# Moving the token transposes into the mixer and cutting the first layer's modulation sums into 128x256 pieces

## The chip, the cores and the metric

One NeuronCore of a Trainium2 chip runs the whole program in one launch. The metric is device time in microseconds (us), the median of three runs. The engines are named as in the profile: PE (TensorE), DVE (VectorE), ACT (ScalarE), POOL (GpSimd) and SP (SyncE, which here issues most of the DMAs). Each engine executes its own list of instructions strictly in order.

## The reference

Two transformer layers work on 256 context tokens and 1024 latent tokens of width 1024, all in float32. The part that the change touches:

```python
x = x + ml[2] * mix_l                      # mix_l = recurrent mixer's output @ w_out
x = x + ml[5] * _conv_ffn(_modulate(_rms(x), ml[3], ml[4]), ffn_w_up[i], ffn_conv[i], ffn_w_down[i])
ctx = ctx + mc[2] * mix_c                  # the same for the context, in the first layer only
ctx = ctx + mc[5] * _conv_ffn(_modulate(_rms(ctx), mc[3], mc[4]), ...)
# ml, mc = split(silu(cond) @ mod_w[i] + mod_b[i], 6): six vectors of 1024 for each condition
```

## The kernel before

The program keeps tokens as columns. Its stages follow each other: a start that normalises the tokens; a **mixer** (four delta-rule heads, four gated-linear heads, up to about 960 us); the **output projection** of the mixer (about 962 to 1111 us); a feed-forward block for the context tokens (`fg<-hx`, from 1115 us); one for the latent tokens; then the second, attention layer. The tokens are cut in three chunks: chunk 0 is the context (256 columns), chunks 1 and 2 are latent (512 columns each).

The order on each engine is not written by hand. The program is recorded in source order, and a scheduler places each instruction by a time line of its own; tile pools (a pool with n buffers of a tag makes the n+1st tile wait for the first one's readers) and true dependencies are its limits.

*Mixer.* Projections (`pj`) fill PE between chains: per delta head `kk` (`pskk`), a 30-step `inverse` on DVE, and `levels` (`py`, `px`, `pxt`: short matmuls with a DVE step between them). `dn_step` walks the recurrence (`p`, `vn`, `r`). `merge(h8)` takes a finished head `o` (`o_d`, from DRAM scratch `o_scr`), squares it on ACT (`msq`), scales it on DVE (`mss`), transposes it on PE (`pmt`), gates it (`mg`) and stores it in `m_scr`. `merge(3)` is the last.

*Output projection* (`if True:` block from L1250). `m_in` loads the merged heads: for chunk 0 straight into `m`, for chunks 1 and 2 through `mt`, split into a high part (ACT, `m1h`, `m2h`) and a low part (DVE, `m1l`, `m2l`). `x_in` loads 128 tokens of 4 KB rows (`st`), transposes them on PE (`xtr`) and copies them into the residual `xT` on ACT and DVE. For each chunk and each of eight output tiles `dt`, a 512 KB weight tile is loaded (`st<-in_rec_w_out_dram`, L1303); chunk 0 multiplies it as it is (`po<-m,st`), chunks 1 and 2 split it (`woh` on ACT, `wol` on POOL) and run three products. DVE adds the result into `xT`. The head order `KORD` puts head 3 last.

*Modulation sums.* After each chunk `mod_acc(mp, pd, "d", 0, (4, 3, 5)[ci], (0, 1), 0, 1024)` computes one of the vectors 4, 3, 5 of layer 0 for both conditions: eight 512 KB weight tiles `mw` are loaded by SP, and DVE multiplies and adds them into two accumulators (`macc`, 128x1024). PE then sums over partitions (`mps`). After chunk 1 `rms_mod` makes `hx`, the context's normalised and modulated input of the feed-forward block: squares (ACT `rm_sq`), sums (DVE `rm_rs`, PE and DVE `rm_cs`), the power on POOL, a diagonal (`rm_dg`), a broadcast matmul, a product (DVE `rm_sq`), and a scale and shift that is dealt out by `scale_shift`: rows 0 to 3 to ACT, 4 and 5 to POOL, 6 and 7 to DVE. The modulation of layer 1 is already done in 128x256 pieces by `mod_chain`, through POOL's DMA queue with six `mw` buffers.

Of the kernel before, what the change touches and what calls it, by code (L numbers as in the profile page):

```python
# [9 lines left out]
F32 = mybir.dt.float32  # L10
# [9 lines left out]
KD = 8  # L20
NCTX = 256
NLAT = 1024
NT = NCTX + NLAT
# [47 lines left out]
def kernel(  # L71
# [33 lines left out]
    def pool(stack, name, bufs, psum=False, side=None):  # L105
        kw = {"space": PSUM} if psum else {}
        return stack.enter_context(tc.tile_pool(name=name, bufs=bufs, reuse_waits="tile", side=side, **kw))
# [33 lines left out]
    m_scr = dr.tile([8, 128, NT], F32, name="m_scr")  # L141
    aq_scr = dr.tile([2, 8, 128, NLAT], F32, name="aq_scr")
    x0_scr = dr.tile([2, 128, KD, NCTX], F32, name="x0_scr")

# [345 lines left out]
    with loop:  # L490
# [248 lines left out]
        def gatef(h8):  # L739
            gate_p(h8, lv, "ktk")  # L740

        bc8 = ac.tile([128, 2, 8], F32, name="bc8")
        dma(bc8[:, 0], dn_dt_bias[0].rearrange("a b -> (a b)").partition_broadcast(128))
# [57 lines left out]
        dn_run(1)  # L801
        kk(1)
        q_tok(1)
        inverse(1)
# [12 lines left out]
        pend += [(1, n) for n in range(NB)]  # L817
        kk(2)
        q_tok(2)
        inverse(2)  # L820
# [14 lines left out]
        dn_run(1)  # L835
        kk(3)
        q_tok(3)
        inverse(3)
# [237 lines left out]
    def load(p, src):  # L1076
        st = p.st.tile([128, KD, 128], F32, tag="st", name="st")
        dma(st, src)
        return st
# [178 lines left out]
    if True:  # L1258
# [4 lines left out]
        with ExitStack() as po:  # L1263
            hC = pool(po, "hC", 1, side="right")
            tmp = pool(po, "tmpc", 1)
            fc.st = pool(po, "fstc", 2)
            fw = Ffn()
            fw.st = pool(po, "fstw", 2)
            mi = pool(po, "mi", 4)
            wo = pool(po, "wo", 5)  # L1270
            mp = pool(po, "mpc", 1)
            mhl = {}
            def x_in(g):
                src = ctx_in[0, g:g + 128] if g < NCTX else x[0, g - NCTX:g - NCTX + 128]
                ci, o = (0, g) if g < NCTX else ((g - NCTX) // 512 + 1, (g - NCTX) % 512)
                xin = load(fc, src.rearrange("p (k m) -> p k m", m=128))
                for hf in range(2):
                    ps = pd.tile([128, 4, 128], F32, tag="d", name="xtr")
                    for k in range(4):
                        T.transpose(ps[:, k], xin[:, hf * 4 + k], ident)  # L1280
                    evac(hf, xT[ci][:, hf * 4:hf * 4 + 4, o:o + 128], ps)

            xs_ = iter(range(0, NT, 128))
            def m_in(ci):
# [7 lines left out]
                for k in KORD:  # L1292
# [3 lines left out]
                    tt(V, ml_[:, k], mt[:, 0:n], mh[:, k].bitcast(F32), ALU.subtract)  # L1296
            for ci in (0, 1, 2):
                m_in(ci)
            for _ in range(6):
                x_in(next(xs_))  # L1300
            for ci in (0, 1, 2):
                t0, n = CHUNKS[ci]
                d = 1 if ci == 0 else 0  # L1303
                if ci not in (0, 1, 2):
                    m_in(ci)
                for dt in range(KD):
# [11 lines left out]
                    stt(V, xT[ci][:, dt], ps[:, 0:n], mcol(0, d, 2)[:, dt:dt + 1], xT[ci][:, dt], ALU.mult, ALU.add)  # L1318
                    for _ in range({(0, d): 1 for d in range(2, 6)}.get((ci, dt), 0)):
                        x_in(next(xs_))  # L1320
                dump(f"xmix{ci}", xT[ci])
                mod_acc(mp, pd, "d", 0, (4, 3, 5)[ci], (0, 1), 0, 1024)
                if ci == 1:
                    hx = h0.tile([128, KD, NCTX], F32, tag="m0l", name="hx")
                    rms_mod(tmp, pd, "d", xT[0], NCTX, mcol(0, 1, 4), mcol(0, 1, 3), hx, None, w=128)
        if stop == "C":
# [356 lines left out]
```

## Time and profile before

| | |
|---|---|
| median of 3 runs (3437.09 to 3443.26) | 3440.48 us |
| the profiled execution's own time | 3433.85 us |
| its span | 3432.1 us |
| PE, DVE, POOL, ACT busy | 93%, 70%, 45%, 38% of the span |
| granted TensorE clock, mean | 0.964 of full speed |

The profile is one execution. "Busy" for PE includes the modelled tail of pipelined matmuls. The page cuts the span in 40 slices of 85.8 us; the slice from 944 us is one of three where PE's digit is 7, and the one where the DMA's is highest (8, 261 GB/s read and written).

### The profile page before, as it was taken

The page shows a single profiled execution, that of the slowest core. Times are in us where ns is not written, and L with a number is a line of the kernel's source. Part 1 is how long each engine was busy: PE and PEld are TensorE (multiplying, and loading weights), DVE is VectorE, ACT ScalarE, POOL GpSimd, SP SyncE. Part 2 cuts the span into 40 slices and gives each one's busy share as a digit, 9 for nine tenths or more (in the row PEclk, how much of TensorE's full clock was granted, in tenths as well). Part 3 has the DMA queues.
Part 4 walks back from the last instruction along what each step waited for, and adds up shares of the span by engine and source line. Part 5 has one row for each costly group of instructions (what it writes and reads, how often), then busy time and mean ns, then how long its engine had stood idle before and what let it go on. Part 6 is the DMA issues. An engine that isn't in the chain of part 4 may idle for free.

```text
span 3432.1 us, 47550 instructions
## 1 busy us (share of the span) xinstructions
PE 3184.6 (93%) x16708; PEld 2661.1 (78%) x16708; DVE 2414.4 (70%) x4177; ACT 1308.3 (38%) x2982; POOL 1542.5 (45%) x1459
## 2 busy tenths in 40 slices
PE   7987988899979999999999988989999799999998
PEld 4776877777768888788888778978788678887877
DVE  5567467568777875777676775577787667777677
ACT  4434233654321222333332324556356433333333
POOL 2232231223215332656555535753554555555554
PEclk9998999999989999999999999999999899999999
DMA  5445444645686664211212121330331011111211
GB/s 184 115 120 161 135 130 133 180 146 171 189 261 191 187 193 135 80 41 53 59 50 59 41 70 59 111 102 26 100 101 35 25 54 51 56 44 53 59 49 71
DMA packets 438508, 350.14 MB, mean 102 GB/s; under 512 B 57556, under 2 KB 385470, under 8 KB 437758
## 3 DMA queue, kind: packets, MB, share of 16 engines
q1 hardware_dynamic: 429054, 321.93, 31.5%
q0 software_dynamic: 9216, 25.18, 2.3%
q8 instruction: 132, 2.16, 0.3%
q14 instruction: 106, 0.87, 0.1%
HBM read 286.25 MB, written 60.76 MB: 101 GB/s over the span
## 4 chain that ended last, share of the span: by engine, by line
PE 64%; DVE 18%; DMA 6%; ACT 4%; POOL 3%; issue 3%; SPq 1%; DVEq 0%; ACTq 0%; POOLq 0%
PE fg L157 6%; PE fg L155 6%; PE fg L156 6%; PE fg L1220 4%; PE fd L156 4%; PE fd L157 4%; PE fd L155 4%; PE fd L1230 2%; DVE st L94 2%; PE pj L155 2%; PE pj L156 2%; PE pj L157 2%; PE apo L155 2%; PE apo L157 2%; PE apo L156 2%
## 5 line engine op out<-in xcount | busy, mean ns | idle before, releaser
L103 DVE SCALAR_TENSOR_TENSOR xT<-fd,mod,xT 128x512 f32<-128x512 f32 (+1 forms) x432 | 291.0, 694 | 201.9 <-PE fd L157 172.7
L155 PE MATMUL pj<-hhi,whi 128*128 128x512 f32 (+1 forms) x696 | 260.9, 375 | 21.2 <-ACT raw L525 13.4
L156 PE MATMUL fd<-gl,dh 128*128 128x512 f32 (+1 forms) x688 | 266.7, 388 | 6.5 <-DVE gl L94 6.4
L157 PE MATMUL fd<-gh,dl 128*128 128x512 f32 (+1 forms) x688 | 266.0, 387 | 0.0
L155 PE MATMUL fd<-gh,dh 128*128 128x512 f32 (+1 forms) x688 | 262.6, 392 | 0.5 <-ACT gh L1155 0.3
L156 PE MATMUL pj<-hlo,whi 128*128 128x512 f32 (+1 forms) x696 | 257.6, 370 | 1.2 <-DVE hlo L94 1.2
L157 PE MATMUL pj<-hhi,wlo 128*128 128x512 f32 (+1 forms) x696 | 257.1, 369 | 0.0
L94 DVE TENSOR_TENSOR st<-st 128x512 f32<-128x512 f32 x176 | 211.1, 1200 | 51.3 <-POOL s1l L94 38.7
L103 DVE SCALAR_TENSOR_TENSOR macc<-mw,sc,macc 128x256 f32<-128x256 f32 (+1 forms) x322 | 212.4, 690 | 28.3 <-DMA mw<-in_mod_w_dram 26.8
L94 POOL TENSOR_TENSOR dl<-sd,dh 128x256 fp32r<-128x256 f32 x168 | 158.7, 960 | 106.0 <-ACT dh L160 105.9
L94 POOL TENSOR_TENSOR wlo<-wst,whi 128x512 fp32r<-128x512 f32 x58 | 76.7, 1322 | 265.2 <-ACT whi L160 259.6
L100 POOL TENSOR_SCALAR P<-P,rc 128x512 f32<-128x512 f32 (+1 forms) x192 | 119.2, 637 | 153.9 <-DVE rc L1541 66.0
L94 POOL TENSOR_TENSOR w0l<-st,w0h 128x1024 fp32r<-128x1024 f32 x44 | 106.0, 2409 | 173.3 <-ACT w0h L1100 121.9
L155 PEld LDWEIGHTS pj<-hhi,whi 128*128 128x128 f32 x696 | 136.3, 196 | 45.2 <-ACT raw L525 15.7
L217 POOL DMA_DIRECT2D mw<-in_mod_w_dram x192 | 105.8, 552 | 139.1 <-DVE macc L103 59.3
L156 PEld LDWEIGHTS fd<-gl,dh 128*128 128x128 f32 x688 | 129.7, 188 | 38.5 <-DVE gl L94 12.1
L94 POOL TENSOR_TENSOR p<-p,u 128x512 f32<-128x512 f32 (+1 forms) x45 | 93.7, 2083 | 145.2 <-DVE u L94 145.2
L1220 PE MATMUL fg<-hx,st 128*128 128x256 f32 x704 | 158.1, 379 | 0.0
L103 DVE SCALAR_TENSOR_TENSOR ft<-fraw,conv_f,ft 128x1024 f32<-128x1024 f32 x88 | 137.2, 1559 | 28.3 <-ACT ft L91 27.5
L155 PEld LDWEIGHTS fd<-gh,dh 128*128 128x128 f32 x688 | 128.6, 189 | 34.3 <-ACT gh L1155 8.3
L156 PEld LDWEIGHTS pj<-hlo,whi 128*128 128x128 f32 x696 | 136.4, 196 | 18.9 <-DVE hlo L94 1.4
L157 PEld LDWEIGHTS pj<-hhi,wlo 128*128 128x128 f32 x696 | 135.9, 195 | 18.3 <-issue 0.2
(610 smaller groups left out, 9867.1 us busy)
## 6 DMA issues: line engine op xcount, KB each, us to landing
st<-in_ffn_w_up_dram SPq DMA_DIRECT2D x88, 512.0 KB
mw<-in_mod_w_dram POOLq DMA_DIRECT2D x192, 128.0 KB, 3.2
st<-in_ffn_w_up_dram SPq DMA_DIRECT2D x88, 256.0 KB
sd<-in_ffn_w_down_dram SPq DMA_DIRECT2D x176, 128.0 KB
sh<-sh_scr SPq DMA_DIRECT2D x80, 256.0 KB
wst<-in_rec_w_in_dram SPq DMA_DIRECT2D x56, 256.0 KB
st<-in_rec_w_out_dram SPq DMA_DIRECT2D x24, 512.0 KB
mw<-in_mod_w_dram SPq DMA_DIRECT2D x24, 512.0 KB
```

The costliest lines, as they stand in the source:

```text
L94: e.tensor_tensor(out=o, in0=a, in1=b, op=op)
L100: e.tensor_scalar(out=o, in0=a, scalar1=s1, scalar2=s2, op0=op0, op1=op1)
L103: e.scalar_tensor_tensor(out=o, in0=a, scalar=s, in1=b, op0=op0, op1=op1)
L155: T.matmul(ps, lhsT=wh, rhs=xh, start=first, stop=False)
L156: T.matmul(ps, lhsT=wh, rhs=xl, start=False, stop=False)
L157: T.matmul(ps, lhsT=wl, rhs=xh, start=False, stop=last)
L217: (eng or nc.sync).dma_start(out=w, in_=mod_w[l, k * 128:(k + 1) * 128, c0:c0 + width])
L1220: T.matmul(ps, lhsT=h[k // 4][:, k % 4], rhs=hx[:, k], start=k == 0, stop=k == KD - 1)
L1230: T.matmul(ps, lhsT=h[i][:, k], rhs=gl[f], start=i == 0, stop=i == len(fs) - 1)
```

## The change

Every 128-token piece of x and ctx is now loaded, transposed and copied inside the mixer, in two halves, and written to a DRAM scratch `xt_scr` (20 pieces: eight are recorded behind `kk(1)`, six behind `kk(2)`, six behind `kk(3)`). Loaded token halves and their transposed copies share the two buffers of tag `ktk` with the mixer's other staging tiles, and the one PSUM buffer `pt`. The output projection then loads `xT` chunk by chunk from `xt_scr`. `m_in(1)` is called ahead of chunk 0, `m_in(2)` and the last `x_in` calls at set points of the loops. The projection's weight pool has four buffers instead of two. The three modulation vectors become twelve pieces of 128x256 in one `mod_chain` on POOL's DMA queue, four steps after each output tile from `dt` 3 of chunk 0 on, the rest behind the loops. `hx` is recorded behind `dt` 3 of chunk 2 instead of behind chunk 1.

```diff
+        xpieces = [(g, hf) for g in range(0, NT, 128) for hf in range(2)]
+        def x_tr(cnt):
+            for _ in range(cnt):
+                g, hf = xpieces.pop(0)
+                src = ctx_in[0, g:g + 128] if g < NCTX else x[0, g - NCTX:g - NCTX + 128]
+                xin = lv.tile([128, 4, 128], F32, tag="ktk", name="xin2")
+                dma(xin, src[:, hf * 512:(hf + 1) * 512].rearrange("p (k m) -> p k m", m=128))
+                ps = pt.tile([128, 4, 128], F32, tag="pt", name="xtr")
+                for k in range(4):
+                    T.transpose(ps[:, k], xin[:, k], ident)
+                xo = lv.tile([128, 4, 128], F32, tag="ktk", name="xo")
+                S.copy(out=xo, in_=ps)
+                dma(xt_scr[:, hf * 4:hf * 4 + 4, g:g + 128], xo)
...
         kk(1)
+        x_tr(8)
         q_tok(1)
...
-            fw.st = pool(po, "fstw", 2)
+            fw.st = pool(po, "fstw", 4)
...
-            def x_in(g):
...
+            def x_in(ci):
+                t0, n = CHUNKS[ci]
                 for hf in range(2):
-                    ps = pd.tile([128, 4, 128], F32, tag="d", name="xtr")
-                    for k in range(4):
-                        T.transpose(ps[:, k], xin[:, hf * 4 + k], ident)
-                    evac(hf, xT[ci][:, hf * 4:hf * 4 + 4, o:o + 128], ps)
+                    dma(xT[ci][:, hf * 4:hf * 4 + 4], xt_scr[:, hf * 4:hf * 4 + 4, t0:t0 + n])
...
-            for ci in (0, 1, 2):
-                m_in(ci)
-            for _ in range(6):
-                x_in(next(xs_))
+            mods = mod_chain([(mp, pd, "d", 0, i, (0, 1), q, 256, 6, nc.gpsimd) for i in (4, 3, 5) for q in range(4)])
+            todo = {(0, 4): lambda: x_in(1), (1, 1): lambda: m_in(2), (1, 4): lambda: x_in(2)}
+            m_in(0)
+            x_in(0)
+            m_in(1)
...
-                    for _ in range({(0, d): 1 for d in range(2, 6)}.get((ci, dt), 0)):
-                        x_in(next(xs_))
+                    todo.get((ci, dt), lambda: None)()
+                    for _ in range(0 if ci == 0 and dt < 3 else 4):
+                        next(mods, None)
+                    if (ci, dt) == (2, 3):
+                        hx = h0.tile([128, KD, NCTX], F32, tag="m0l", name="hx")
+                        rms_mod(tmp, pd, "d", xT[0], NCTX, mcol(0, 1, 4), mcol(0, 1, 3), hx, None, w=128)
                 dump(f"xmix{ci}", xT[ci])
-                mod_acc(mp, pd, "d", 0, (4, 3, 5)[ci], (0, 1), 0, 1024)
-                if ci == 1:
-                    hx = h0.tile([128, KD, NCTX], F32, tag="m0l", name="hx")
-                    rms_mod(tmp, pd, "d", xT[0], NCTX, mcol(0, 1, 4), mcol(0, 1, 3), hx, None, w=128)
+            for _ in mods:
+                pass
```

What the scheduler makes of it shows in the engines' lists. First DVE, at the end of the output projection, before the change; `xT_9032` is the residual of chunk 2, `xT_9042` the context's residual, from which `hx` is made:

```order
L103 SCALAR_TENSOR_TENSOR xT_9032<-po,mod_71,xT_9032 128x512
L103 SCALAR_TENSOR_TENSOR macc<-mw,sc,macc 128x1024
L94 TENSOR_TENSOR rm_sq<-xT_9042,rm_ps 128x1024 x2
L103 SCALAR_TENSOR_TENSOR macc<-mw,sc,macc 128x1024 x2
L100 TENSOR_SCALAR hx<-rm_sq,mod_72 128x128 x2
L103 SCALAR_TENSOR_TENSOR xT_9032<-po,mod_71,xT_9032 128x512
L100 TENSOR_SCALAR hx<-rm_sq,mod_72 128x128 x2
L103 SCALAR_TENSOR_TENSOR macc<-mw,sc,macc 128x1024 x2
L103 SCALAR_TENSOR_TENSOR xT_9032<-po,mod_71,xT_9032 128x512
```

These are the first three of chunk 2's eight updates, and `hx` stands between them. DVE now, from the eighth and last update of chunk 2 (`xT_9233`) on:

```order
L103 SCALAR_TENSOR_TENSOR xT_9233<-po,mod_71,xT_9233 128x512
L94 TENSOR_TENSOR mod_71<-mps,modb 128x2
L94 TENSOR_TENSOR mod_72<-mps,modb 128x2
L103 SCALAR_TENSOR_TENSOR macc<-mw,sc,macc 128x256 x2
L100 TENSOR_SCALAR rm_cs<-rm_ps 128x1
L170 TENSOR_REDUCE rm_rs<-rm_sq 128x128 x2
L100 TENSOR_SCALAR rm_cs<-rm_ps 128x1
L103 SCALAR_TENSOR_TENSOR macc<-mw,sc,macc 128x256 x4
L98 TENSOR_SCALAR macc<-mw,sc 128x256 x2
L103 SCALAR_TENSOR_TENSOR macc<-mw,sc,macc 128x256 x14
L98 TENSOR_SCALAR macc<-mw,sc 128x256 x2
L98 TENSOR_SCALAR rm_dg<-ident,rm_cs 128x128 x2
```

In the nine rows that follow stand the product and DVE's part of `hx`, with six more `macc` in between; all of them have moved from ahead of chunk 2's second update to behind its last. On POOL the same place read before:

```order
L94 TENSOR_TENSOR wol<-st,woh 128x1024 x13
L176 TENSOR_TENSOR rm_cs<-rm_cs,nhalf 128x1 x2
L94 TENSOR_TENSOR wol<-st,woh 128x1024
L100 TENSOR_SCALAR hx<-rm_sq,mod_72 128x128 x4
L94 TENSOR_TENSOR wol<-st,woh 128x1024 x2
L217 DMA mw<-in_mod_w_dram 128x256 x22
```

And it reads now (the rows ahead of these hold sixteen `wol` and, in groups of one to three between them and 21 at their head, the first 57 loads of `mw`):

```order
L94 TENSOR_TENSOR wol<-st,woh 128x1024
L218 DMA mw<-in_mod_w_dram 128x256 x29
L177 TENSOR_TENSOR rm_cs<-rm_cs,nhalf 128x1 x2
L218 DMA mw<-in_mod_w_dram 128x256 x12
L100 TENSOR_SCALAR hx<-rm_sq,mod_72 128x128 x4
L218 DMA mw<-in_mod_w_dram 128x256 x20
```

The power and POOL's part of `hx` have moved behind the last `wol` and behind 86 and 98 loads of `mw`. Last, PE between the mixer's end and the output projection, before:

```order
L897 MATMUL pmt<-ident,o_g 128x128 x2
L1280 MATMUL xtr<-ident,st 128x128 x32
L897 MATMUL pmt<-ident,o_d 128x128 x4
L1280 MATMUL xtr<-ident,st 128x128 x8
L897 MATMUL pmt<-ident,o_d 128x128 x4
L1280 MATMUL xtr<-ident,st 128x128 x8
L897 MATMUL pmt<-ident,o_d 128x128 x2
L1280 MATMUL xtr<-ident,st 128x128 x8
L1311 MATMUL po<-m_9067,st 128x256 x14
```

and now:

```order
L433 MATMUL p_7175<-r,dd 128x128
L437 MATMUL p_7179<-vn,kd 128x128
L438 MATMUL p_7179<-vn,dd 128x128
L916 MATMUL pmt<-ident,o_d 128x128 x10
L1322 MATMUL po<-m_9265,st 128x256 x48
L231 MATMUL mps<-ones,macc 128x128 x4
```

The token transposes are gone from here, and the ten transposes of `merge(3)` follow the recurrence's last matmuls directly. Of the 48 `po` the first twelve use the other heads; the thirteenth is the first that needs head 3.

## Rows read from the trace of the kernel before

**Rows 1.** Busy time by stretch: stretch and its length, five engines, granted clock, DMA share, GB/s

```profile
200.00:930.00 730.00, 650.24 (x4002) 547.42 (x4001) 497.64 (x1141) 295.16 (x786) 205.68 (x220) 0.96 0.51 148
930.00:1009.50 79.50, 58.00 (x280) 48.84 (x279) 49.01 (x76) 22.88 (x69) 5.48 (x5) 0.81 0.87 282
1009.50:1115.00 105.50, 103.34 (x458) 84.53 (x458) 85.78 (x92) 22.32 (x27) 57.69 (x42) 0.94 0.67 193
```

**Rows 2.** PE in order of time: start, length, instructions, idle before and releaser

```profile
962.93 6.21 PE L1311 MATMUL po<-m,st 128*128 128x256 f32 x28
969.31 1.03 PE L1311 MATMUL po<-m,st 128*128 128x256 f32 x4
977.25 10.17 PE L1311 MATMUL po<-m,st 128*128 128x256 f32 x32 [6.37 <-DMA st<-in_rec_w_out_dram]
999.07 3.69 PE L1311 MATMUL po<-m,st 128*128 128x256 f32 x16 [0.43 <-DMA st<-in_rec_w_out_dram]
1012.41 0.79 PE L157 MATMUL po<-m1h,wol 128*128 128x512 f32 x1 [2.16 <-POOL wol L94]
```

**Rows 3.** SP's DMA issues in order of time, last merge

```profile
941.64 0.42 SPq L84 DMA_DIRECT2D o_d<-o_scr  x1
```

**Rows 4.** ACT and DVE in order of time, last merge

```profile
948.08 0.31 ACT L880 ACTIVATE msq<-o_d 128x128 f32<-128x128 f32 x1 [0.37 <-DMA o_d<-o_scr]
960.83 0.47 DVE L103 SCALAR_TENSOR_TENSOR mg<-pmt,nrmc,mg 128x256 f32<-128x256 f32 x1
```

**Rows 5.** PE in order of time, end of chunk 2

```profile
1111.31 0.39 PE L157 MATMUL po<-m2h,wol 128*128 128x512 f32 x1
1111.54 3.63 PE L230 MATMUL mps<-ones,macc 128*128 128x1 f32 x32
1115.03 7.15 PE L1220 MATMUL fg<-hx,st 128*128 128x256 f32 x32
```

**Rows 6.** DVE in order of time, output projection

```profile
1017.54 6.62 DVE L103 SCALAR_TENSOR_TENSOR macc<-mw,sc,macc 128x1024 f32<-128x1024 f32 x2 [1.19 <-DMA mw<-in_mod_w_dram]
1079.23 2.34 DVE L94 TENSOR_TENSOR rm_sq<-xT,rm_ps 128x1024 f32<-128x1024 f32 x2
1083.89 0.65 DVE L100 TENSOR_SCALAR hx<-rm_sq,mod 128x128 f32<-128x128 f32 x2
1092.49 2.46 DVE L103 SCALAR_TENSOR_TENSOR macc<-mw,sc,macc 128x1024 f32<-128x1024 f32 x2
1102.49 2.46 DVE L103 SCALAR_TENSOR_TENSOR macc<-mw,sc,macc 128x256 f32<-128x256 f32 x6
1116.05 0.74 DVE L103 SCALAR_TENSOR_TENSOR xT<-po,mod,xT 128x512 f32<-128x512 f32 x1
1118.61 1.91 DVE L169 TENSOR_REDUCE rm_rs<-rm_sq 128x128 f32<-128x1024 f32 x1
```

**Rows 7.** POOL in order of time, output projection

```profile
1017.33 2.40 POOL L94 TENSOR_TENSOR wol<-st,woh 128x1024 fp32r<-128x1024 f32 x1 [2.19 <-ACT woh L160]
1080.55 0.90 POOL L100 TENSOR_SCALAR hx<-rm_sq,mod 128x128 f32<-128x128 f32 x2 [4.18 <-DVE rm_sq L94]
1081.67 3.03 POOL L100 TENSOR_SCALAR hx<-rm_sq,mod 128x128 f32<-128x128 f32 x2 [0.23 <-DVE rm_sq L94]
1104.56 0.54 POOL L217 DMA_DIRECT2D mw<-in_mod_w_dram  x1 [0.25 <-DVE macc L103]
```

**Rows 8.** PE in order of time: token transposes, and the recurrence's last steps

```profile
943.26 1.09 PE L1280 MATMUL xtr<-ident,st 128*128 128x128 f32 x8 [1.67 <-DMA st<-in_x_dram]
932.30 0.80 PE L436 MATMUL p<-vn,kd 128*128 128x128 f32 x2 [0.93 <-ACT vn L434]
935.97 0.80 PE L436 MATMUL p<-vn,kd 128*128 128x128 f32 x2 [0.35 <-ACT vn L434]
```

**Rows 9.** Busy time by stretch, as in Rows 1: a wait of the mixer, the chunks' border

```profile
300.00:320.00 20.00, 10.28 (x43) 8.42 (x41) 18.36 (x43) 8.71 (x26) 6.01 (x3) 0.66 0.35 111
1060.00:1070.00 10.00, 10.00 (x45) 8.79 (x45) 5.45 (x11) 1.05 (x1) 5.82 (x4) 0.66 0.59 178
```

More of the change, by code (lines that the diff above doesn't have):

```diff
@@ L142 @@
     aq_scr = dr.tile([2, 8, 128, NLAT], F32, name="aq_scr")
+    xt_scr = dr.tile([128, KD, NT], F32, name="xt_scr")
     x0_scr = dr.tile([2, 128, KD, NCTX], F32, name="x0_scr")
@@ L818 @@
         kk(2)
+        x_tr(6)
         q_tok(2)
@@ L836 @@
         kk(3)
+        x_tr(6)
         q_tok(3)
@@ L1265 @@
             tmp = pool(po, "tmpc", 1)
-            fc.st = pool(po, "fstc", 2)
             fw = Ffn()
-            fw.st = pool(po, "fstw", 2)
+            fw.st = pool(po, "fstw", 4)
             mi = pool(po, "mi", 4)
@@ L1272 @@
             mhl = {}
-            def x_in(g):
-                src = ctx_in[0, g:g + 128] if g < NCTX else x[0, g - NCTX:g - NCTX + 128]
-                ci, o = (0, g) if g < NCTX else ((g - NCTX) // 512 + 1, (g - NCTX) % 512)
-                xin = load(fc, src.rearrange("p (k m) -> p k m", m=128))
+            def x_in(ci):
+                t0, n = CHUNKS[ci]
                 for hf in range(2):
-                    ps = pd.tile([128, 4, 128], F32, tag="d", name="xtr")
-                    for k in range(4):
-                        T.transpose(ps[:, k], xin[:, hf * 4 + k], ident)
-                    evac(hf, xT[ci][:, hf * 4:hf * 4 + 4, o:o + 128], ps)
-            xs_ = iter(range(0, NT, 128))
+                    dma(xT[ci][:, hf * 4:hf * 4 + 4], xt_scr[:, hf * 4:hf * 4 + 4, t0:t0 + n])
             def m_in(ci):
@@ L1303 @@
                 d = 1 if ci == 0 else 0
-                if ci not in (0, 1, 2):
-                    m_in(ci)
                 for dt in range(KD):
```

## Prediction

> **What bounds the kernel now.** I read the busy time by stretch first. In the mixer from 200 to 930 us PE is busy for 650 of 730 us; around the last merge and chunk 0 it is busy for 58.0 of 79.5 us, at a granted clock of 0.81 and with the DMA engines 87% busy; from chunk 1 to the start of the context's feed-forward block it is busy for 103.3 of 105.5 us [rows 1]. So only the middle stretch, 930 to 1009.5 us, loses much, and there the DMA engines are what is short. PE in order of time shows how: chunk 0 runs in short pieces between waits for its weights (6.37 us before the piece at 977.25), part of them at the slow clock: 32 instructions in 10.17 us against 16 in 3.69 us, which is 0.231 us each and the fast rate [rows 2]. The last merge feeds it: its `o_d` is asked for at 941.64 [rows 3], is on chip at 948.08, and its last gating ends at 961.30 [rows 4]. At the other end of the stage there is no gap: chunk 2's last matmul starts at 1111.31, 32 small `mps` follow, and `fg` begins at 1115.03 [rows 5], because `hx` was made during chunk 2.
>
> **The start of the output projection.** The change takes the token loads out of the last merge's surroundings, puts four weight tiles on chip instead of two, and asks for far fewer modulation weights before chunk 1: 21 loads of 128 KB stand ahead of the first `wol` in POOL's list, where SP issued ten of 512 KB. Counted from the issue of `o_d`: before, PE was through chunk 0 and out of its first wait in chunk 1 at 1012.41, 70.8 us later [rows 2, 3]. After: from `o_d` to the last gating it took 19.7 us; without transposes of tokens in between and with `o_d` landing sooner I take 14. The store of that head and its load back took about 8 us (961.30 to the piece at 969.31 that uses it); four new loads of `xT`, 4.2 MB, stand ahead of them, 15 us at the 282 GB/s of this stretch [rows 1], but they are issued with `o_d` and so are nearly through; I take 6. By then twelve of chunk 0's 64 matmuls are done, and the other 52 (104 instructions) take 24.0 us at 0.231, the `mps` piece 0.9, and a slow start costs 2.8 (10.17 less 2 x 3.69). That is 47.7 us, a gain of 23.1. The bounds: if the DMA stays the limit, only the 2.5 MB of modulation weights that are no longer asked for are saved, 9 us; if all goes well and the clock does not fall, 26. I take 21, near the upper end because the weights of four output tiles now wait on chip.
>
> **The border of the chunks.** At 1060 to 1070 us the clock was granted at 0.66 although PE was busy throughout, right behind 32 `mps` of one column [rows 9]. Those are now of 128 columns and spread. I count 3 us won (10 x 0.34), between 0 and 3.
>
> **The end of the output projection.** Here is the largest loss, and it follows from the order alone. DVE's whole way to `hx` now stands behind the last update of chunk 2, which can't run before PE's last matmul E; before, it stood ahead of chunk 2's second and third update. PE has nothing between but twelve `mps` and the four matmuls of the norm, and then `fg`, which needs `hx`. DVE's work behind E, one after the other: the update 0.74; two `mod` 0.3 and two `macc` of 128x256 at 0.41 (2.46 for 6), 0.8; the two sums of the next norm, 1.91 each, 3.8, with two `rm_cs` at 0.3 together; 22 `macc` 9.0; `rm_dg` 0.6; then the product 2.34 with two `macc` and two `mod` around it 1.1, two more `macc` 0.8, and four pieces of `hx` 1.3 with two `macc` 0.8 between: 21.9 us [rows 6]. POOL ends later still. Its part of `hx` stands behind 98 loads of `mw`; with six buffers the 98th can be issued when 92 steps, 184 `macc`, are done, and DVE has done 176 at its last piece of `hx`: eight more, 3.3 us, then an issue of 0.54 us and POOL's own four pieces, 0.90 to 3.03 us for two [rows 7]. That gives E + 28, against E + 3.6 before: 24 us of waiting. After it PE starts slowly, as at 977.25: 2. Sum 26; the lower bound is 18 (POOL's part early, and the first four products of `fg` done before it comes), the upper 33 (both pairs on POOL at 3.03, loads of `mw` late).
>
> **The mixer.** 20 pieces bring 80 transposes to PE, eight in 1.09 us [rows 8], so 10.9 us if PE had no room; ACT gets 20 copies and SP 40 issues beside work that does not fill them. PE has 80 us of room [rows 1], but six of the pieces stand between the short matmuls of `levels`, where each delay goes on down the chain. Between 0 and 18 (10.9, and 1.2 us for each of those six); I take 6, as rather more than half of the pieces stand among projections.
>
> **The recurrence's tail.** Behind the last projection matmul PE's list now holds six steps of the recurrence instead of four and a half; a step takes 3.7 us there (932.30 to 935.97 [rows 8]), a part of which is only moved. 3, between 0 and 6.
>
> **Sum**: -21 - 3 + 26 + 6 + 3 = +11 us, made against the profiled execution's 3433.85, so 3444.9. The median of the runs shown lies 6.6 us above that execution, so the median to expect is 3440.48 + 11, rounded 3451 us.
>
> **A rule weighed.** Two `macc` of 128x1024 took 2.46 us together at 1092.49, away from POOL's subtractions, and 6.62 at 1017.54, beside a `wol` of 2.40 us that had begun at 1017.33 [rows 6, 7]. The Trainium skill, "SBUF — State Buffer", section "Who interferes with whom", says of this pair that a DVE instruction with two SBUF inputs contends with a GpSimd one that reads SBUF, and that the loser fully blocks until the other is through. The trace agrees. By that rule, cutting the pieces to a quarter does not cut what a `wol` costs DVE, and makes it likelier that a piece waits. What this would give by the rows is the third rival.
>
> **The rivals.** (1) The order that the scheduler found for the mixer is better by chance. Place: the waits for `inverse`, as at 300 to 320 us, where PE worked 10.3 of 20 us at a clock of 0.66 [rows 9]. In PE's list some more projection work stands in the first such wait now, but less in the second, which speaks against it. Were 10 us of such waiting filled, the mixer and its tail would give -10 in place of +9, and the sum -8: 3432. It is faster than before from the point where mixer and tail together save 2 us. (2) The pieces in `levels` choke on their two buffers: load, copy and store of a piece must pass before the next, PE waits for the load, and SP holds back what stands behind a store. At 2 us more for six pieces, +12: 3463. For it speaks that they share `ktk` and `pt` with the other staging tiles; against it that a level's own matmuls leave some 3 us between. (3) `wol` blocks DVE: sixteen of 2.4 us are 38 us in the 96 us of chunks 1 and 2; 49 modulation steps of 0.82 and 16 updates of 0.74 need 52 of the 58 that are left, so nothing falls behind, but if the waits cluster, DVE comes to E about 8 us late: 3459. (4) The change does not do at the start what it says, and the loads of `xT` hold back the last merge as the tokens did: 9 instead of 21 won, 3463.
>
> **Chances.** The forecast 0.45, rival 1 0.27, 2 0.10, 3 0.08, 4 0.10. A difference under 0.2% (6.9 us) can't be told from no change. Around +11 with some 9 us either way, the forecast is slower 0.65, the same 0.33, faster 0.02 of its share; rival 1 at -8 is faster 0.65, the same 0.30; the others are slower at 0.95. Together: slower 0.57, the same 0.24, faster 0.19. The range takes in rival 1 with a few us to spare (-12, which is also all terms but the last gap at their good ends) and the dear rivals (+28): 3428 to 3468. The forecast's own is 3442 to 3460.
>
> **What would show it.** In the changed kernel: PE idle for more than 15 us between the last `po` of chunk 2 and a running `fg`, ended by `hx` from POOL or DVE, and `rm_cs` on POOL behind a row of `mw`; chunk 0 in one run at 0.23 us with no wait for weights over 2 us; about 48 us from the issue of `o_d` to chunk 1; the last merge's `o_d` asked for 5 to 15 us later than 941.64. If `fg` starts within 8 us of chunk 2's end, the main loss is wrong and the kernel is faster; if `o_d` is asked for earlier than before, the mixer's term is wrong.

## The result and the profile after

The changed kernel takes 3461.92 us (median of 5 runs, 3454.27 to 3464.17) against 3437.09 us before (5 runs in all): 1.0063 times as long, 95% interval 1.005 to 1.0077, which is 17 to 26 us. The forecast was 3451 and slower, the range 3428 to 3468. The direction and the place of the main loss came out, its size in part by luck; the sum was 10 to 14 us too small. The time alone would not have told the forecast from its rivals: 3461.92 lies just above the forecast's own 3442 to 3460 and beside the 3459 and 3463 of rivals 2 to 4. The rows do.

The profiled execution took 3464.17 us. Set against the profile of before, each point read from the timelines (last `pj` or recurrence instruction, the issue of the last `o_d`, chunk 1's first matmul with `wol`, the end of chunk 2, the first and the last `fg<-hx`), the difference splits like this:

| stretch | before, us | after, us | difference | forecast |
|---|---|---|---|---|
| start to the mixer's last projection | 920.4 | 933.8 | +13.4 | +6 |
| from there to the recurrence's last step | 16.8 | 19.3 | +2.5 | +3 |
| from there to the issue of `o_d` | 4.4 | 9.3 | +4.9 | none |
| `o_d` to chunk 1 | 70.8 | 51.6 | -19.2 | -21 |
| chunk 1 to the end of chunk 2 | 99.3 | 100.1 | +0.8 | -3 |
| end of chunk 2 to `fg` | 3.3 | 28.3 | +25.0 | +24 |
| context block | 233.3 | 240.9 | +7.6 | +2 (slow start) |
| the rest of the program | 2083.8 | 2079.1 | -4.7 | 0 |

The sum is +30.3, by these two executions; the one of the changed kernel is the slowest of its five. Busy time by stretch, after (stretch and its length, five engines, granted clock, DMA share, GB/s), for [rows 1]:

```profile
200.00:930.00 730.00, 651.20 (x4000) 553.85 (x3998) 485.62 (x1128) 299.40 (x788) 210.01 (x217) 0.94 0.54 157
930.00:1011.00 81.00, 53.35 (x272) 43.09 (x271) 42.84 (x102) 23.30 (x77) 18.79 (x30) 0.81 0.96 301
1011.00:1114.00 103.00, 97.10 (x435) 78.93 (x434) 91.56 (x149) 19.49 (x19) 73.34 (x80) 0.98 0.50 151
1114.00:1142.40 28.40, 6.48 (x34) 5.91 (x33) 26.84 (x67) 3.19 (x8) 16.48 (x29) 0.58 0.52 155
```

A new stretch has appeared: in the last row PE works 6.5 of 28.4 us, while DVE works 26.8. PE in order of time shows the front and the end, for [rows 2] and [rows 5]:

```profile
974.54 1.08 PE L916 MATMUL pmt<-ident,o_d 128*128 128x128 f32 x4 [21.42 <-DVE o_d L94]
...
979.69 23.80 PE L1322 MATMUL po<-m,st 128*128 128x256 f32 x96 [0.58 <-DVE mg L103]
1003.33 1.05 PE L231 MATMUL mps<-ones,macc 128*128 128x128 f32 x8
1004.22 7.07 PE L1322 MATMUL po<-m,st 128*128 128x256 f32 x32
...
1113.96 1.05 PE L231 MATMUL mps<-ones,macc 128*128 128x128 f32 x8
...
1127.12 1.20 PE L231 MATMUL mps<-ones,macc 128*128 128x128 f32 x4 [11.60 <-DVE macc L103]
...
1140.56 2.04 PE L231 MATMUL mps<-ones,macc 128*128 128x128 f32 x8 [10.32 <-DVE macc L103]
1142.39 7.92 PE L1239 MATMUL fg<-hx,st 128*128 128x256 f32 x28
1149.71 13.98 PE L1239 MATMUL fg<-hx,st 128*128 128x256 f32 x64
```

Chunk 0 now runs from 979.69 to 1011.3 without a wait for weights. But PE stands idle for 21.4 us before it, and for two waits of 11.6 and 10.3 us before `fg`. DVE in order of time says what it did meanwhile, for [rows 6]:

```profile
1114.16 0.75 DVE L103 SCALAR_TENSOR_TENSOR xT<-po,mod,xT 128x512 f32<-128x512 f32 x1 [0.76 <-PE po L158]
...
1115.99 3.64 DVE L170 TENSOR_REDUCE rm_rs<-rm_sq 128x128 f32<-128x1024 f32 x2
...
1121.75 5.62 DVE L103 SCALAR_TENSOR_TENSOR macc<-mw,sc,macc 128x256 f32<-128x256 f32 x14
...
1129.30 2.34 DVE L94 TENSOR_TENSOR rm_sq<-xT,rm_ps 128x1024 f32<-128x1024 f32 x2
...
1133.82 0.59 DVE L100 TENSOR_SCALAR hx<-rm_sq,mod 128x128 f32<-128x128 f32 x2
1134.40 6.41 DVE L103 SCALAR_TENSOR_TENSOR macc<-mw,sc,macc 128x256 f32<-128x256 f32 x16
```

The norm is finished only at 1129 to 1134, with sums for the third modulation vector in between, as its order had said. The last line is not in the forecast: `hx` is complete at 1134.4, but eight `mps` instructions of the third vector stand ahead of `fg` in PE's list, and wait for these 16 `macc`. The forecast had named the twelve `mps` in this place (24 instructions) and let them wait for nothing.

SP's waits in 1085 to 1145 us (what waited, on what, total, times, longest), and its issues in the last merge, for [rows 3]:

```profile
SPq L84 <- DVE hx L100: 68.2, 1, 68.2
```

```profile
947.85 2.98 SPq L84 DMA_DIRECT2D mg<-gate_scr  x1
950.87 3.11 SPq L84 DMA_DIRECT2D st<-in_rec_w_out_dram  x2
954.08 2.43 SPq L84 DMA_DIRECT2D m_scr<-mg  x2
956.60 0.41 SPq L84 DMA_DIRECT2D o_scr<-o_dn  x1
...
962.45 0.32 SPq L84 DMA_DIRECT2D o_d<-o_scr  x1
...
1133.15 11.28 SPq L84 DMA_DIRECT2D st<-in_ffn_w_up_dram  x11
```

`o_dn` was ready at 953.5. Its store stood in SP's list behind the five issues shown ahead of it, which held SP for 8.7 us. The context block's first weights are asked for at 1133.15, after a wait of 68.2 us for `hx`.

### The profile page after: what moved, and what is told of

It reads as the page before. It is cut to its first block, busy times and chain, and to the rows that moved or that the text cites. A ratio compares the mean times of both kernels' runs of the same rounds, so it can differ in the third digit from the quotient of the medians.

```text
span 3462.4 us, 47996 instructions
## 1 busy us (share of the span) xinstructions
PE 3181.8 (92%) x16708; PEld 2662.3 (77%) x16708; DVE 2442.1 (71%) x4341; ACT 1313.8 (38%) x2992; POOL 1588.3 (46%) x1555
## 5 line engine op out<-in xcount | busy, mean ns | idle before, releaser
L103 DVE SCALAR_TENSOR_TENSOR macc<-mw,sc,macc 128x256 f32<-128x256 f32 x448 | 243.5, 579 | 17.0 <-DMA mw<-in_mod_w_dram 15.3
L218 POOL DMA_DIRECT2D mw<-in_mod_w_dram x288 | 159.3, 553 | 193.3 <-DVE macc L103 90.0
L94 POOL TENSOR_TENSOR dl<-sd,dh 128x256 fp32r<-128x256 f32 x168 | 157.1, 950 | 107.2 <-ACT dh L161 106.6
L156 PEld LDWEIGHTS pj<-hhi,whi 128*128 128x128 f32 x696 | 138.2, 198 | 39.0 <-ACT raw L526 13.5
```

Source lines behind the costliest of these rows:

```text
L94: e.tensor_tensor(out=o, in0=a, in1=b, op=op)
L103: e.scalar_tensor_tensor(out=o, in0=a, scalar=s, in1=b, op0=op0, op1=op1)
L156: T.matmul(ps, lhsT=wh, rhs=xh, start=first, stop=False)
L218: (eng or nc.sync).dma_start(out=w, in_=mod_w[l, k * 128:(k + 1) * 128, c0:c0 + width])
```

## The experiments

Each was timed in five rounds against the kernel before. The differences in us are the ratio's, at 3437.5 us.

| kernel | median, us | ratio, 95% interval | difference |
|---|---|---|---|
| changed kernel | 3461.92 | 1.0063, 1.005 to 1.0077 | +22 |
| norm early | 3449.76 | 1.0034, 1.0022 to 1.0045 | +12 |
| sums only | 3440.59 | 1.0006, 0.9997 to 1.0014 | +2 |
| tokens only | 3427.86 | 0.9979, 0.9968 to 0.9989 | -7 |
| no transposes | 3451.70 | 1.0046, 1.0031 to 1.006 | +16 |
| tokens in the projection | 3429.10 | 0.9975, 0.9966 to 0.9984 | -9 |
| two weight buffers | 3436.00 | 0.9996, 0.9987 to 1.0006 | -1 |
| pieces first | 3506.43 | 1.0203, 1.0183 to 1.0222 | +70 |
| all tokens before chunk 0 | 3420.40 | 0.9953, 0.9939 to 0.9967 | -16 |
| one transpose of four | 3423.98 | 0.9956, 0.9943 to 0.9969 | -15 |
| norm's buffers apart | 3442.73 | 1.0019, 1.001 to 1.0028 | +7 |
| norm early, buffers apart | 3445.74 | 1.0024, 1.0014 to 1.0035 | +8 |

The same points in their profiles, in us of each run:

| kernel | last projection | recurrence ends | `o_d` asked | chunk 1 | chunk 2 ends | `fg` | block ends | from there to the end |
|---|---|---|---|---|---|---|---|---|
| before | 920.4 | 937.2 | 941.6 | 1012.4 | 1111.7 | 1115.0 | 1348.3 | 2083.8 |
| changed | 933.8 | 953.1 | 962.4 | 1014.0 | 1114.1 | 1142.4 | 1383.3 | 2079.1 |
| norm early | 928.1 | 948.3 | 956.9 | 1009.3 | 1112.5 | 1120.8 | 1368.0 | 2080.2 |
| sums only | 926.2 | 942.0 | 948.0 | 1018.0 | 1118.4 | 1118.2 | 1358.5 | 2082.0 |
| tokens only | 933.5 | 953.1 | 962.2 | 1014.6 | 1116.5 | 1119.8 | 1354.8 | 2081.7 |
| no transposes | 920.5 | 937.3 | 944.1 | 993.2 | 1099.3 | 1121.0 | 1361.2 | 2087.9 |
| tokens in the projection | 925.1 | 940.9 | 947.6 | 1001.0 | 1107.7 | 1111.0 | 1344.3 | 2080.3 |
| two weight buffers | 932.0 | 951.6 | 957.0 | 1018.2 | 1116.8 | 1120.1 | 1355.1 | 2075.7 |
| pieces first | 1005.1 | 1019.4 | 1030.0 | 1082.2 | 1184.4 | 1187.7 | 1422.7 | 2091.8 |
| all tokens before chunk 0 | 923.3 | 938.3 | 945.8 | 996.2 | 1103.4 | 1106.7 | 1341.7 | 2072.8 |
| one transpose of four | 926.5 | 943.0 | 949.9 | 1001.6 | 1101.9 | 1105.2 | 1340.2 | 2078.0 |
| norm's buffers apart | 926.8 | 951.9 | 959.7 | 1016.2 | 1109.4 | 1109.3 | 1348.0 | 2091.8 |
| norm early, buffers apart | 933.6 | 957.5 | 966.7 | 1021.6 | 1116.3 | 1116.1 | 1356.9 | 2092.6 |

An end of chunk 2 is the modelled end of its last matmul, so `fg` can stand 0.2 us ahead of it.

The last column is the part that no edit names, and it is not constant. Behind the context block PE runs the same instructions in the same order in the changed kernel, tokens only, two weight buffers, one of four and all tokens before chunk 0, and takes 2072.8 to 2081.7 us for them, so some 9 us are the execution's own. In the two kernels with the buffers apart and in pieces first it has another order in common, and takes 2091.8 to 2092.6. The order of before is a third, 2083.8 in its one profile. So an edit can move the time behind it by way of the scheduler's order, and a few us of a median can lie there.

### Each half alone

Sums only: the kernel before, with

```diff
+            mods = mod_chain([(mp, pd, "d", 0, i, (0, 1), q, 256, 6, nc.gpsimd) for i in (4, 3, 5) for q in range(4)])
...
+                    for _ in range(0 if ci == 0 and dt < 3 else 4):
+                        next(mods, None)
+                    if (ci, dt) == (2, 3):
+                        hx = ...; rms_mod(...)
-                mod_acc(mp, pd, "d", 0, (4, 3, 5)[ci], (0, 1), 0, 1024)
```

> The kernel before with only the modulation sums in small pieces, spread as in the changed kernel, and hx issued where the changed kernel issues it; tokens are loaded and transposed in the projection as before, two weight buffers. Theory: the mixer is as before, o_d is asked for within 3 us of 941.6; chunk 0 gains up to 10 us by the modulation weights that are no longer loaded there; hx stands ahead of the last updates in this order, so the gap before fg is under 12 us; 3428 to 3442. Rival (the small pieces are what costs, by weight subtractions that block the vector engine): chunk 1 and 2 longer by 8 us or more or a gap of 15 us, 3448 or more.

Tokens only: the changed kernel with its modulation sums and `hx` put back as they were before.

> The changed kernel with the modulation sums and hx issued as before (three blocks of 512 KB loads, hx after chunk 1): the tokens' transposes in the mixer and the loads by chunk alone. Theory: the mixer stays 13 to 16 us longer and o_d is asked for 15 to 21 us later than 941.6; from o_d to chunk 1 50 to 62 us instead of 70.8; no gap at fg; 3436 to 3450. Rival (the mixer's lateness is an accident of the order that goes with the sums): o_d is asked for within 8 us of 941.6, and the time is 3425 or less.

Of the first expectation the time and the gap came out; `o_d` was asked for 6.3 us later than 941.6 instead of within 3, although its mixer runs in the order of before, and the front won nothing. Alone the small sums cost nothing that can be told from no change (+2), and the tokens win 7 us; together they cost 22. So 27 us belong to the two together and to neither. The table shows where. In the sums-only kernel 70.0 us pass between `o_d` and chunk 1, in the changed kernel 51.6: there the sums have 18 us less before chunk 2 ends, and the order puts `hx` behind it. In the sums-only kernel `hx` was made from 1103.1 to 1109.6, more than 8 us ahead of `fg`. That the shorter front is the reason is read from the table and was not tried by itself (the kernel without transposes, with a front of 49.1 us and nothing added to the mixer, has a gap of 21.7 as well); that `hx` behind chunk 2 is the larger part of the price is shown by the next three kernels. A forecast for each edit alone would have missed it; the order of the whole had it.

The tokens' stretches came as expected (`o_d` asked for 20.6 us later than before, 52.3 us from there to chunk 1, 3.3 us of gap), the time did not: 3427.86 is below the 3436 to 3450 expected, and not the rival's 3425 either. Its profiled execution took 3438.28, 10 us above its own median, and ends the context block 6.5 us later than before, so where the 7 us of the median were won isn't shown. Single profiles are only rough on the mixer. The six profiles with 80 transposes in the mixer have the last projection at 926.8 to 933.8, mean 931.3; the five with none in it at 920.4 to 926.2, mean 923.1: 8 us for the projections, and 13.5 us (952.6 against 939.1) for the recurrence's end. Up to 925 us PE, DVE and ACT run the same instructions in the same order in all six (but for two or three of some 4700 on PE), so the 7 us between them are not the order's.

### The norm's place, and its memory

```diff
-                    if (ci, dt) == (2, 3):
-                        hx = ...; rms_mod(...)
+                    if (ci, dt) == (1, 0):
+                        nsq = []
+                        for q0 in (0, 128):
+                            r, sq = normalised(tmp, pd, "d", xT[0][:, :, q0:q0 + 128])
+                            tt(V, sq, xT[0][:, :, q0:q0 + 128], r, ALU.mult)
+                            nsq.append(sq)
+                    if (ci, dt) == (2, 5):
+                        hx = ...; scale_shift(...) of both halves
```

> The changed kernel, with the context's norm taken out of the far end: its statistics, its matmuls and the product xT times norm are issued after chunk 1's first output tile, and only the last multiply-add with the modulation (hx) after chunk 2's sixth. Theory (the place of the norm behind the modulation sums makes the 28.7 us between chunk 2's last matmul and fg): that gap falls to 4 to 12 us, everything ahead of it stays, and the time goes from 3462 to 3438 to 3446. Rival (the vector engine is behind with its modulation sums in any case; the order of the norm only decides where the lateness shows): gap 15 us or more, or the gap shrinks and the context block is longer by as much; 3455 or more.

The gap fell from 28.3 to 8.3 us, in the expected range; the time fell by 12 us (10 by the ratios) to 3449.76, less than to the expected 3438 to 3446. What came in its place stands in PE's and SP's rows of this kernel (SP's wait in 1085 to 1145 us):

```profile
1112.30 1.05 PE L231 MATMUL mps<-ones,macc 128*128 128x128 f32 x8
1120.79 16.65 PE L1239 MATMUL fg<-hx,st 128*128 128x256 f32 x64 [7.43 <-DMA st<-in_ffn_w_up_dram]
```

```profile
SPq L84 <- DVE hx L100: 54.1, 1, 54.1
```

```profile
1117.35 14.14 SPq L84 DMA_DIRECT2D st<-in_ffn_w_up_dram  x14
```

Now the up weights are late. SP asks for them at 1117.35, while DVE reads its last `hx` out of `rm_sq` (from 1116.7): the context block's weight tiles lie in memory that the norm's buffers had. The block itself took 247.2 us, 14 more than before; its first 64 matmuls 16.65 us, where the changed kernel's second 64 took 13.98. One word moves the norm's buffers to the other side of SBUF:

```diff
-            tmp = pool(po, "tmpc", 1)
+            tmp = pool(po, "tmpc", 1, side="right")
```

> The changed kernel with one word more: the pool of the norm's buffers (tmpc, with rm_sq) lies on the other side of SBUF, so that the feed-forward block's weights do not come to lie on it, and the pools behind it move down. In the order that follows, the sums start in the last merge, half of hx stands ahead of the last update but two, the other half ahead of the last but one. Theory (what the small pieces cost is their place: hx behind chunk 2, and the block's weights waiting 68 us for hx because they lie on rm_sq): the gap between chunk 2 and fg is under 8 us, the up weights are asked for before 1100, and the time is 3428 to 3442. Rival (the small pieces cost by their number: products of ones, POOL's issues, subtractions that block the vector engine): the gap closes but chunk 1 and 2 or the context block are longer by 10 us or more; 3448 or more.

The same word in the kernel with the norm early:

> The kernel with the norm taken out of the far end (3450), and its buffers on the other side of SBUF too. Its 7.4 us wait for up weights goes, and hx stands ahead of the last four updates. By the first theory of the kernel beside it 3428 to 3440, equal to that one within 6 us, since the norm's place then no longer matters; by its rival 3444 or more.

In the kernel with that one word SP waits in 1085 to 1145 us for `wol` and for `fg` itself, not for `hx`, and PE goes straight from chunk 2 into `fg`:

```profile
SPq L84 <- PE fg L1239: 38.8, 17, 15.2
SPq L84 <- POOL wol L94: 17.6, 1, 17.6
```

```profile
1085.76 37.93 SPq L84 DMA_DIRECT2D st<-in_ffn_w_up_dram  x18
```

```profile
1109.03 0.39 PE L158 MATMUL po<-m2h,wol 128*128 128x512 f32 x1
1109.26 2.75 PE L1239 MATMUL fg<-hx,st 128*128 128x256 f32 x12
```

The gap is gone, and of the +22 us 15 with it; the median of 3442.73 is just above the expected 3428 to 3442, below the rival's 3448. With the norm early as well nothing more is won: 3445.74 lies above the 3440 expected and in the range that its rival named (3444 or more). The rival's places are missed in both: chunks 1 and 2 take 93.2 and 94.7 us, shorter than before, and the block 238.7 and 240.8, 5.4 and 7.5 longer. In both, half of `hx` or more stands ahead of chunk 2's last updates, so these two kernels don't show the memory alone.

What is left of the loss sits elsewhere. `o_d` to chunk 1 takes 56.5 and 54.9 us instead of 51.6, since the sums begin in the last merge. But at the end of the context block the kernel with one word more, 1348.0, is level with before, 1348.3. The 8 us that its profile is longer lie behind the block, in the other order: PE's waits of `mps` for `macc` from 1348 us on, in this kernel and before:

```profile
PE mps L231 <- DVE macc L103: 7.5, 4, 3.8
PE mps L230 <- DVE macc L103: 2.0, 3, 1.1
```

### What the token pieces cost the mixer

```diff
         def x_tr(cnt):
-            for _ in range(cnt):
-                ...
+            pass
...
-                    dma(xT[ci][:, hf * 4:hf * 4 + 4], xt_scr[:, hf * 4:hf * 4 + 4, t0:t0 + n])
+                        dma(xT[ci][:, hf * 4:hf * 4 + 4], x[0, t0 - NCTX:t0 - NCTX + n, hs].rearrange("(k p) m -> p k m", p=128))
```

> The changed kernel without its 20 token pieces in the mixer (no loads, transposes, copies and stores there; xT is loaded from the tokens themselves, untransposed, so this part of the computation is left out); the same bytes are loaded in the projection. Theory (the pieces cost the mixer their time on the tensor engine and delays in its chains): o_d is asked for 12 to 20 us sooner than in the changed kernel's 962.4, and the time is 3440 to 3450. Rival (the mixer's order came out worse by itself, the pieces lie in its waits): o_d within 5 us of 962.4, 3457 or more.

The mixer is as long as before to the microsecond (920.5 and 937.3), and `o_d` is asked for 18.3 us sooner than in the changed kernel, as the theory says. The time gained only 6 us by the ratios, 10 by the medians, to just above the expected 3440 to 3450. The far end took most of the rest: chunks 1 and 2 last 106.1 us instead of 100.1, and 21.7 us of gap stay before `fg`, 11.9 of them in one wait for `rm_dg`. Without the pieces PE's list in the mixer is that of before, so this kernel can't tell the pieces' own time from the order that came with them.

```diff
-                for k in range(4):
-                    T.transpose(ps[:, k], xin[:, k], ident)
+                T.transpose(ps[:, 0], xin[:, 0], ident)
...
-                S.copy(out=xo, in_=ps)
+                S.copy(out=xo, in_=ps[:, 0:1].to_broadcast([128, 4, 128]))
```

> The tokens-only kernel (3428) with one transpose in place of four in each of the 20 pieces; load, copy of the same size and store stay, so that three quarters of the transposition are left out. If the tensor engine's time is what the pieces cost the mixer (10.9 us for 80, 2.7 for 20), o_d is asked for 6 to 10 us sooner than 962.2, and the time is 3418 to 3423. If the waits around a piece (for its load, its two buffers) are the cost, o_d stays within 4 us and the time at 3425 or more.

`o_d` came 12.3 us sooner than in the profile of tokens only, and the time fell by 8 us by the ratios, 4 by the medians; 60 transposes of 0.136 us are 8.2. Both figures lie just outside what was expected (6 to 10 us, 3418 to 3423), and on the side of PE's time rather than of the waits. But the mixer's order differs from the tokens-only kernel's too, so that most of the pieces' cost is PE's time is likely and not shown, and how much the waits around a piece add stays open.

```diff
+        x_tr(20)
         k_tok(0)
...
-        x_tr(8)
...
-        x_tr(6)
...
-        x_tr(6)
```

> The tokens-only kernel (3428) with all 20 token pieces issued together near the mixer's start, ahead of the first head's k_tok, instead of 8, 6 and 6 ahead of q_tok of the later heads, so that none stands between the short matmuls of levels. If the pieces cost by standing in the chains of levels, o_d is asked for 6 us or more sooner than 962.2 and the time is 3422 or less; if they cost their 10.9 us of tensor engine time wherever they stand, o_d stays at 956 to 964 and the time at 3424 to 3432.

Both expectations missed: 70 us longer. Its order put twelve of the pieces next to each other, and PE's and SP's rows show what a piece costs then (waits of 100 to 215 us, and SP in order of time):

```profile
PE xtr L753 <- DMA xin<-in_x_dram: 33.8, 12, 3.2
```

```profile
164.70 0.34 SPq L84 DMA_DIRECT2D xin<-in_x_dram  x1
165.35 0.37 SPq L84 DMA_DIRECT2D xt_scr<-xo  x1
168.39 0.34 SPq L84 DMA_DIRECT2D xin<-in_x_dram  x1
169.43 0.37 SPq L84 DMA_DIRECT2D xt_scr<-xo  x1
172.28 0.34 SPq L84 DMA_DIRECT2D xin<-in_x_dram  x1
```

One piece each 3.7 to 3.9 us: its load waits for a buffer that the store or the transposes before it must leave, and PE waits for the load. These waits are 34 of the 70 us; another 10 lie behind the context block (2091.8 us there, 2081.7 in tokens only), and where the rest went stays open. This is the second rival's mechanism, real as soon as pieces follow each other; spread as in the changed kernel it cost 4.6 us of waiting for `xin` in all.

### What makes the front shorter

```diff
-            fw.st = pool(po, "fstw", 4)
+            fw.st = pool(po, "fstw", 2)
```

> The tokens-only kernel (3428) with two buffers for the projection's weights instead of four. If four weight tiles waiting on chip make part of the gain in front, chunk 0 waits for weights again: from o_d to chunk 1 58 us or more instead of 52, 3433 or more. If the order of the token loads makes all of it, 3426 to 3430.

Chunk 0 took 41.0 us instead of 30.7, 8.3 of the difference in four waits for weights, 61.3 us passed between `o_d` and chunk 1, as expected, and the time rose by 6 to 8 us to that of before: without the four buffers the tokens' part wins nothing.

```profile
PE po L1321 <- DMA st<-in_rec_w_out_dram: 8.3, 4, 3.7
```

The next kernel leaves the mixer alone and keeps the transposes in the projection:

```diff
+            fw.st = pool(po, "fstw", 4)
...
-            for ci in (0, 1, 2):
-                m_in(ci)
-            for _ in range(6):
+            m_in(0)
+            for _ in range(2):
                 x_in(next(xs_))
+            m_in(1)
...
+                    if (ci, dt) == (1, 1):
+                        m_in(2)
+                    for _ in range(1 if ci < 2 and 2 <= dt < 6 else 0):
+                        x_in(next(xs_))
```

> The kernel before, its modulation sums and hx untouched, with only the order of loads and the weight buffers of the changed kernel: tokens are loaded chunk by chunk (128 tokens at a time, transposed on the tensor engine in the projection as before), m_in of chunk 2 after chunk 1's second tile, four weight buffers. Nothing is added to the mixer. Theory (the gain of 18 to 22 us in front comes from the order of loads, and the 13 to 16 us lost in the mixer from the pieces there): o_d asked for within 6 us of 941.6, 50 to 58 us from there to chunk 1, up to 5 us more in chunk 1 for 32 transposes; 3415 to 3425, below the tokens-only kernel's 3428. Rival (the gain in front needs the tokens already transposed, since the loads through the tensor engine hold back the projection as before): 65 us or more from o_d to chunk 1, 3433 or more.

From `o_d` to chunk 1 53.4 us, as with tokens transposed ahead; chunks 1 and 2 take 106.7, 4.8 more than with tokens only. At 3429.10 it is level with that kernel, not below it at 3415 to 3425 as expected. The last version brings all ten groups ahead of chunk 1, where PE waits for the merge:

```diff
             m_in(0)
-            for _ in range(2):
+            for _ in range(6):
                 x_in(next(xs_))
             m_in(1)
+            for _ in range(4):
+                x_in(next(xs_))
```

> The kernel with tokens loaded chunk by chunk and transposed in the projection (3429), with all ten token groups loaded and transposed ahead of chunk 0 and around m_in of chunk 1, where the tensor engine waits for the last merge, instead of four of them in chunk 1 (4.3 us of transposes). If the hole before chunk 0 has room, chunks 1 and 2 are 4 us shorter, from o_d to chunk 1 stays at 53 to 56 us, and the time is 3422 to 3428. If the loads ahead of chunk 0 are what costs there, as in the kernel before, 60 us or more from o_d to chunk 1 and 3432 or more.

At 3420.40 it is the fastest of all: 0.9953 times before (0.9939 to 0.9967), below the 3422 to 3428 expected. But it did not get there as expected. Chunks 1 and 2 take 107.2 us, not 4 less than the 106.7 of the kernel beside it, and of the 10 us between the two profiles 7.5 lie behind the context block, where PE's list is the same but for four instructions. So where most of its gain over that kernel comes from isn't shown. What the rows show is the front: it takes 50.4 us, though more is loaded there, and transposes fill what had been PE's wait of 21.4 us in the changed kernel:

```profile
953.70 1.94 PE L1280 MATMUL xtr<-ident,st 128*128 128x128 f32 x8 [2.58 <-DMA st<-in_x_dram]
955.92 1.94 PE L1280 MATMUL xtr<-ident,st 128*128 128x128 f32 x8 [0.27 <-DMA st<-in_x_dram]
```

## Why the prediction was right, and where its sum was not

**The gap before `fg`** (+24 forecast, +25.0): right in place and cause, `hx` behind chunk 2; that the size came out to 1 us was in part luck. DVE's part of `hx` was done at 1134.4, E + 20, as forecast (E + 21.9). POOL's, which was to end the wait at E + 28, was done at 1133.2, E + 19 (its rows follow, for [rows 7]), since its loads of `mw` were not as late as reckoned. The last 8 us, to `fg` at E + 28.3, were PE's own list: eight `mps` instructions of the third vector ahead of `fg`, which the sum had at nothing. And a second wait lay hidden under the first, the block's weights: with the norm early, PE's wait of 7.43 us ended with them. What would be late next, once `hx` was early, had not been asked.

```profile
1130.62 0.89 POOL L100 TENSOR_SCALAR hx<-rm_sq,mod 128x128 f32<-128x128 f32 x2 [0.37 <-DVE rm_sq L94]
1131.74 1.49 POOL L100 TENSOR_SCALAR hx<-rm_sq,mod 128x128 f32<-128x128 f32 x2 [0.23 <-DVE mod L94]
```

**The front** (-21, -19.2): right; tokens by chunk make it and need the four buffers, while the sums alone changed it by under 1 us (70.0), so the lower bound that rested on modulation weights no longer loaded named the wrong saver.

**The mixer and the tail** (+6 and +3): this is the term that was mis-sized. In the pair of profiles it was 13.4 and 2.5, over all profiles 13.5 together. That is the 10.9 us of transposes and a little more, where 6 was taken because PE had room; whether by their time or by the order that came with them stays open. With the next term, `o_d` was asked for 20.8 us later, outside the 5 to 15 that were to be the sign. A reading of this, not tried: PE's 80 us of idle time in [rows 1] are waits inside chains, which come again behind a piece.

**The issue of `o_d`** was counted as following the tail. It came 4.9 us later still: the store of `o_dn` was issued 3.1 us after `o_dn` was ready, behind SP's other issues, where before the change it had been issued at once, and from the store to the issue of `o_d` it took 5.9 us instead of 4.0.

**The border** (-3, +0.8): the gain that was forecast is there, and a wait that was not forecast took it. The 32 `mps` of one column, before, and then 1060 to 1070 us after:

```profile
1059.12 4.33 PE L230 MATMUL mps<-ones,macc 128*128 128x1 f32 x32
```

```profile
1060.00:1070.00 10.00, 10.00 (x49) 8.21 (x48) 7.72 (x12) 2.10 (x2) 7.71 (x8) 1.00 0.60 185
```

The granted clock is 1.00 there, where [rows 9] had 0.66. But PE lost 5 us at 1030 to a new wait. PE's, DVE's and POOL's rows there:

```profile
1030.01 2.05 PE L231 MATMUL mps<-ones,macc 128*128 128x128 f32 x8 [5.07 <-DVE macc L103]
```

```profile
1011.27 7.61 DVE L103 SCALAR_TENSOR_TENSOR macc<-mw,sc,macc 128x256 f32<-128x256 f32 x8
...
1019.38 0.17 DVE L98 TENSOR_SCALAR mod<-mod 128x2 f32<-128x2 f32 x1
...
1019.64 2.67 DVE L98 TENSOR_SCALAR mod<-mod 128x2 f32<-128x2 f32 x1
...
1026.78 3.48 DVE L103 SCALAR_TENSOR_TENSOR macc<-mw,sc,macc 128x256 f32<-128x256 f32 x4
```

```profile
1010.99 2.35 POOL L94 TENSOR_TENSOR wol<-st,woh 128x1024 fp32r<-128x1024 f32 x1 [1.37 <-ACT woh L161]
...
1014.99 2.41 POOL L94 TENSOR_TENSOR wol<-st,woh 128x1024 fp32r<-128x1024 f32 x1
...
1019.85 2.43 POOL L94 TENSOR_TENSOR wol<-st,woh 128x1024 fp32r<-128x1024 f32 x1
...
1024.09 4.68 POOL L94 TENSOR_TENSOR wol<-st,woh 128x1024 fp32r<-128x1024 f32 x2
```

Eight pieces took 7.61 us, against 0.41 each alone [rows 6]: 4.3 us more, beside 4.8 us of `wol`; the four from 1026.78 took 3.48, beside 4.68 of `wol`. So cutting the sums did not cut what a `wol` costs DVE: the third rival's mechanism at 5 us, not its 8 late ones. The Trainium skill, "SBUF — State Buffer", section "Who interferes with whom", says that a DVE instruction with two SBUF inputs contends with a GpSimd one that reads SBUF; the trace agrees in these rows. (The section calls the port that the two share an exclusive lock; its words "fully blocks", which the prediction took over, are said there of DVE's 2-port modes.)

**The context block** (+7.6) had only its slow start in the sum, 2 us (28 matmuls in 7.92 us after the idle stretch; all `fg` of the block were busy 2.5 us longer). Left out was that it takes over sums that are late: its `mps` are busy for 14.1 us instead of 11.3, and PE waits 2.5 us in it, where it had not waited. The sums-only kernel, with no idle stretch ahead of the block, shows the same 7 us (240.3).

**The rest of the program** was taken as unchanged, and it was not the same list: PE's order behind the block differs from that of before (-4.7 by these profiles).

**Rivals.** The first (a better mixer order) fell: no kernel with the pieces ended its projections before 926.5, against 920.4. The second and third are real mechanisms at smaller prices. The fourth fell: 19.2 us were won at the front, not 9, and `o_d` landed 5.5 us after its issue, 6.4 before.

**The range.** Its lower end was said to be all terms but the last gap at their good ends, -12. Those add up to -3 (-26 - 3 + 26), and to -11 with the gap at its 18 as well.

## What to carry to other kernels

Read an edit to a scheduled kernel from the order of the whole, since two edits that cost nothing and gain apart can lose together: here, as the tables read, the shorter front took away the time that the sums had needed. When a buffer's last reader moves later, ask which later tile lies on its memory, because that tile's loads move with it. Compare stretches, and look at the part that the edit doesn't touch as well: here it moved by up to 20 us. Put added PE work where PE waits for something that doesn't depend on it (with 80 transposes in and around the wait before chunk 0 the front took 50.4 us, without any 49.1; in the mixer they came with about 13 us).

## What the runs showed of the hardware

PE's clock after a wait: in 1114 to 1142.4 us the granted clock was 0.58, in the 7.6 us behind it 0.77, then 1.00; the first 28 `fg` took 0.283 us each, the next 64 0.218. An instruction's size did not protect it from a subtraction on POOL: the operation on `mod` (128x2) shown above at 1019.64 took 2.67 us beside a `wol` of 2.43, the same one at 1019.38 0.17. And the mixer's projections ended up to 7 us apart in single executions of the same order (926.8 to 933.8), so that a term of some us there needs several profiles or a timed kernel.
